# The first MLP layer of a one-core transformer block as seven half-block products for eight

## The chip, the cores and the metric

The kernel runs as one program on one core of a Trainium2 chip. The time is the device time of one execution, in microseconds (us). Five engines work side by side, each with its own queue of instructions in a fixed order: TensorE (PE, the matrix products; PEld is its loading of weights), VectorE (DVE), ScalarE (ACT), GpSimd (POOL) and SyncE (SP), which here only issues DMAs. They wait for each other by semaphores. An instruction that waits holds up all that stands behind it on its engine.

## The reference

One layer of a diffusion backbone: 1024 latent tokens of 1024 features, 256 context tokens. Two mixers (a gated long convolution by a Fourier transform, and retention with eight heads) read the same normed and modulated input, their outputs go through one output projection, and an MLP with a squared ReLU of 4096 hidden features follows:

```python
hx = _modulate(_rmsnorm(x, norm1_g[l]), mx[0][:, None], mx[1][:, None])
ux = hx @ w_in[l]
mix_x = _token_mixers(ux, rope, s_f, s_b, *mixer_w)
x_new = x + mx[2][:, None] * (mix_x @ w_out[l])
hx2 = _modulate(_rmsnorm(x_new, norm2_g[l]), mx[3][:, None], mx[4][:, None])
x_new = x_new + mx[5][:, None] * _sq_relu_mlp(hx2, w_mlp1[l], w_mlp2[l])
return _rmsnorm(x_new, norm_f_g)

def _sq_relu_mlp(h, w1, w2):
    return jnp.square(jax.nn.relu(h @ w1)) @ w2
```

Inputs and outputs are float32.

## The kernel before

Features lie on the 128 partitions, tokens along the free axis; a tile of 128 features by 1024 tokens is 4096 bytes of each partition. Every large operand is split into two float32r parts, the nearest 12-bit part (hi, by a cast on ScalarE) and the rest (lo, by a subtraction on VectorE). A product is then three matmuls (mm3, lines 174 to 177): hi by hi, hi by lo, lo by hi. The moving operand has 512 tokens, the stationary one is a 128 x 128 piece of the weights.

Around the change the work goes in four stages.

1. q, the last piece of the input projection (pq, until 566 us). It reads hxh and hxl, the split input.
2. The output projection. Its convolution share (out_conv, poh0 to poh7) reads mxh and mxl, which split_mix makes from mix_d, eight loads into two buffers mraw of 512 tokens each (lines 1042 to 1048). Its pieces stand between the steps of the retention. The retention share (por) reads mrh and mrl, first for tokens 0 to 511, then for the rest. After each half the second norm follows: squares, a sum over the partitions by TensorE (ptr), a root, a broadcast by TensorE (pb, rB), then modulation into h2h and h2l (lines 1186 to 1219).
3. Layer 1 of the MLP, in 16 blocks f of 256 hidden features: 2 x 128 features, 2 halves of the tokens, 8 pieces of the sum and 3 matmuls, 96 in all. Squared ReLU from PSUM gives fh and fl.
4. Layer 2, interleaved with it: block f of the hidden features times 8 output pieces, 96 matmuls, added to XN, the residual, by one VectorE instruction per output piece. Weights come in slabs of 2048 columns, alternately for layers 1 and 2, by prefetch(). The last block works in token parts of 512, 256 and 256, and the final norm follows part by part.

A scheduler orders the instructions of each engine from the order in which they were written; `with urgent()` moves those within it ahead by a fixed amount. Pools are taken from two stacks of SBUF, a left one from low addresses up and a right one from the top down. A tile that takes the place of an earlier one waits for the last reader of that. In bytes of a partition: hxh and hxl lie at 60,512 to 126,048, h2h and h2l at 89,184 to 154,720, mxh and mxl at 163,808 to 196,576, mrh and mrl at 196,576 to 229,344, fh and fl at 188,384 to 221,152.

In the names of instructions, wr_ and wh_, wl_ are a weight slab raw and split (m: MLP, o: output projection), mod2 the gates and shifts.

## Time and profile before

| | |
|---|---|
| three runs, us | 1441.08, 1443.73, 1448.71; median 1443.73 |
| profiled execution, span, us | 1444.2 (no other time is given for it) |
| busy: PE, DVE, ACT, POOL | 1395.0, 870.6, 393.0, 28.3 us |
| matmuls of PE, listed | 7158 |
| mean granted TensorE clock | 0.982 of full speed |
| DMA | 164.77 MB, mean 114 GB/s |

The span is cut into stages by the timelines: the MLP runs from about 712 to 1427 us, half of the whole. Busy times of PE are sums of matmuls that overlap at their ends, so what one costs in a row of many is read from the distance of two starts. A granted clock of 1.00 is 2.4 GHz, 0.50 is 1.2 GHz.

### The profile page before, as it was taken

The page shows a single profiled execution, that of the slowest core. Times are in us where ns is not written, and L with a number is a line of the kernel's source. Part 1 is how long each engine was busy: PE and PEld are TensorE (multiplying, and loading weights), DVE is VectorE, ACT ScalarE, POOL GpSimd, SP SyncE. Part 2 cuts the span into 40 slices and gives each one's busy share as a digit, 9 for nine tenths or more (in the row PEclk, how much of TensorE's full clock was granted, in tenths as well). Part 3 has the DMA queues.
Part 4 walks back from the last instruction along what each step waited for, and adds up shares of the span by engine and source line. Part 5 has one row for each costly group of instructions (what it writes and reads, how often), then busy time and mean ns, then how long its engine had stood idle before and what let it go on. Part 6 is the DMA issues. An engine that isn't in the chain of part 4 may idle for free.

```text
span 1444.2 us, 17943 instructions
## 1 busy us (share of the span) xinstructions
PE 1395.0 (97%) x7158; PEld 1164.4 (81%) x7158; DVE 870.6 (60%) x1365; ACT 393.0 (27%) x600; POOL 28.3 (2%) x36
## 2 busy tenths in 40 slices
...
GB/s 370 154 153 178 223 191 169 105 207 177 131 140 229 150 228 256 241 142 104 44 15 59 37 51 53 35 59 44 44 59 44 44 59 36 53 51 37 59 15 117
DMA packets 80690, 164.77 MB, mean 114 GB/s; under 512 B 8928, under 2 KB 39264, under 8 KB 80352
## 3 DMA queue, kind: packets, MB, share of 16 engines
...
q0 software_dynamic: 1152, 4.19, 0.7%
...
## 4 chain that ended last, share of the span: by engine, by line
PE 83%; DVE 7%; DMA 5%; ACT 2%; issue 1%; SPq 0%; POOL 0%; DVEq 0%; POOLq 0%; ACTq 0%
PE pm L177 15%; PE pm L176 15%; PE pm L175 15%; PE px L175 2%; PE px L176 2%; PE px L177 2%; PE pga L397 1%; DMA dft_f_k<-in_dft_f 1%; PE pGv L900 1%; PE pq L176 1%; PE pq L177 1%; PE pq L175 1%; PE poh L176 1%; PE poh L177 1%; PE poh L175 1%
## 5 line engine op out<-in xcount | busy, mean ns | idle before, releaser
L1295 DVE SCALAR_TENSOR_TENSOR XN<-pm,mod,XN 128x1024 f32<-128x1024 f32 x120 | 154.0, 1283 | 118.3 <-PE pm L177 118.2
L175 PE MATMUL pm<-fh,wh_m 128*128 128x512 f32 (+1 forms) x528 | 205.2, 389 | 0.3 <-DVE XN L1284 0.2
L177 PE MATMUL pm<-fh,wl_m 128*128 128x512 f32 (+1 forms) x528 | 205.4, 389 | 0.0
L176 PE MATMUL pm<-fl,wh_m 128*128 128x512 f32 (+1 forms) x528 | 204.9, 388 | 0.0
L196 ACT CAST wh_m<-wr_m 128x1024 fp32r<-128x1024 f32 x64 | 67.2, 1050 | 457.8 <-PE pm L176 334.4
L197 DVE TENSOR_TENSOR wl_m<-wr_m,wh_m 128x1024 fp32r<-128x1024 f32 x64 | 78.1, 1221 | 169.9 <-ACT wh_m L196 169.8
L176 PE MATMUL pm<-h2l,wh_m 128*128 128x512 f32 x448 | 174.4, 389 | 0.0
L177 PE MATMUL pm<-h2h,wl_m 128*128 128x512 f32 x448 | 174.3, 389 | 0.0
L175 PE MATMUL pm<-h2h,wh_m 128*128 128x512 f32 x448 | 174.3, 389 | 0.0
L175 PEld LDWEIGHTS pm<-fh,wh_m 128*128 128x128 f32 x528 | 99.1, 188 | 23.5 <-DVE XN L1284 0.7
L177 PEld LDWEIGHTS pm<-fh,wl_m 128*128 128x128 f32 x528 | 99.1, 188 | 22.8 <-issue 0.2
L176 PEld LDWEIGHTS pm<-fl,wh_m 128*128 128x128 f32 x528 | 99.1, 188 | 22.6
L175 PEld LDWEIGHTS pm<-h2h,wh_m 128*128 128x128 f32 x448 | 84.1, 188 | 17.7
L176 PEld LDWEIGHTS pm<-h2l,wh_m 128*128 128x128 f32 x448 | 84.1, 188 | 17.5
L177 PEld LDWEIGHTS pm<-h2h,wl_m 128*128 128x128 f32 x448 | 84.1, 188 | 17.5
L1238 DVE TENSOR_TENSOR rl<-rl 128x1024 f32<-128x1024 f32 (+1 forms) x36 | 39.5, 1101 | 78.9 <-ACT fh L1237 78.9
L175 PE MATMUL px<-hxh,wh_x 128*128 128x512 f32 x128 | 50.7, 396 | 0.0
L176 PE MATMUL px<-hxl,wh_x 128*128 128x512 f32 x128 | 50.7, 396 | 0.0
L712 DVE SCALAR_TENSOR_TENSOR adac<-adaw,cs,adac 128x512 f32<-128x512 f32 x56 | 43.0, 767 | 12.7 <-DMA adaw<-in_w_ada 12.0
L177 PE MATMUL px<-hxh,wl_x 128*128 128x512 f32 x128 | 50.5, 394 | 0.0
L1236 ACT ACTIVATE rl<-pm 128x1024 f32<-128x1024 f32 x28 | 28.7, 1026 | 57.1 <-PE pm L177 57.1
L177 PE MATMUL pk<-wh_k,hxl 128*128 128x256 f32 x128 | 39.6, 310 | 3.2 <-DVE hxl L438 3.2
...
## 6 DMA issues: line engine op xcount, KB each, us to landing
wr_m<-in_w_mlp SPq DMA_DIRECT2D x64, 512.0 KB, 3.5
adaw<-in_w_ada SPq DMA_DIRECT2D x64, 256.0 KB, 4.0
wa<-in_w_ada SPq DMA_DIRECT2D x16, 512.0 KB, 10.2
...
xr<-in_x SPq DMA_DIRECT2D x8, 512.0 KB, 7.2
eo_d<-eo POOLq DMA_DIRECT2D x8, 512.0 KB, 4.3
...
```

The costliest lines, as they stand in the source:

```text
L175: PE.matmul(o, lhsT=lh, rhs=rh, start=first, stop=False)
L176: PE.matmul(o, lhsT=lh, rhs=rl, start=False, stop=False)
L177: PE.matmul(o, lhsT=ll, rhs=rh, start=False, stop=last)
L196: A.copy(wh[:, ks], raw)
L197: V.tensor_tensor(wl[:, ks], raw, wh[:, ks].bitcast(F32), op=ALU.subtract)
L397: PE.matmul(pga[h][0:4, n, :], lhsT=cv[:, k, :], rhs=w_[:, n * 512:(n + 1) * 512], start=(k == 0), stop=(k == KC - 1 and i == 1))
L712: V.scalar_tensor_tensor(ac, wa, cs[:, k, 0:1], ac, op0=ALU.mult, op1=ALU.add)
L900: PE.matmul(o, lhsT=y[:, 0, cb], rhs=iv[:, sl[0]], start=True, stop=False)
L1236: A.activation(rl, ps, AF.Relu)
L1238: V.tensor_tensor(rl, rl, rl, op=ALU.mult)
L1295: V.scalar_tensor_tensor(xn[d], ps.rearrange("p a n -> p (a n)"), gate2[:, d:d + 1], xn[d], op0=ALU.mult, op1=ALU.add)
```

## The change

Layer 1 becomes a product of 2 x 2 blocks. For each f the weights are cut by hidden half (128 features of the first 2048, 128 of the second) and by half of the sum; the activations by half of the sum and by half of the tokens. With A11, A12, A21, A22 for the weights and B11 to B22 for the activations, seven products stand for eight:

- 1: A11 B11; 2: A12 B21; 5: (A21 + A22) T1 with T1 = B12 - B11; 6: (S5 - A11) T2 with S5 = A21 + A22 and T2 = B22 - T1; 3: (A12 - S6) B22; 7: (A11 - A21) T3 with T3 = B22 - B12; 4: A22 T4 with T4 = B21 - T2.

Each is 4 pieces of the sum by 3 matmuls. The weights' sums are made once per f (w1_prep), the tokens' once (b11 to t4, 16,384 bytes each, at 19,552 to 153,568). Copies of PSUM (s1, s5, s2) and additions (join) put the four blocks of the output together. The squared ReLU is stored unsplit to DRAM (h_d). When layer 1 is done, layer 2 loads it back and splits it, in 8 groups of four chunks of 128 hidden features.

Beside this: the second half of the tokens goes through the output projection in two parts of 256; the modulation is done in place in XN, so XN is stored to DRAM (x_d) and loaded again for layer 2; XN moves to the right stack at 196,576, mxh and mxl to 89,184 to 121,952, mrh and mrl to 56,416 to 89,184, hidden tiles to 19,552 to 85,088.

The diff, cut to its core (removed code of the MLP and comments left out):

```diff
+    xnp = opool("xnp", side="right")
+    XN = xnp.tile([P, KC, T], F32, tag="XN", name="XN")
     xn = [XN[:, k] for k in range(KC)]
-    mxr = opool("mxr", side="right")
-    mxp = opool("mxp", side="right")
+    mxr = opool("mxr")
+    mxp = opool("mxp")
...
+    w1p = opool("w1p", side="right")
+    raws = {}
+
+    def w1_load(f):
+        raw = w1p.tile([P, KC, 2, P], F32, tag="raw", name=f"w1r{f}")
+        for h in range(2):
+            SP.dma_start(raw[:, 4 * h:4 * h + 4], I["w_mlp1"][f][:, 4 * h:4 * h + 4])
+        a11, a12, a21, a22 = raw[:, 0:4, 0], raw[:, 4:8, 0], raw[:, 0:4, 1], raw[:, 4:8, 1]
+        raws[f] = dict(a11=a11, a12=a12, a21=a21, a22=a22)
...
+    def w1_split(f, p, a):
+        t = w1[f, p] = w1p.tile([P, 2, 4, P], F32R, tag=f"w{p}", name=f"w1{p}_{f}")
+        split(t[:, 0], t[:, 1], raws[f][a])
+
+    def w1_sum(f, p, a, b, op):
+        r = raws[f]
+        t = w1p.tile([P, 4, P], F32, tag="sum", bufs=3, name=f"w1s{p}_{f}")
+        V.tensor_tensor(t, r[a], r[b], op=op)
+        r[p] = t
+        w1_split(f, p, p)
...
+    b0p = opool("b0p", side="right")
+    n2p = opool("n2p", side="right")
+    B = {}
+
+    def b_tile(pool, key):
+        B[key] = pool.tile([P, 2, 4, 512], F32R, name=f"B_{key}")
+        return B[key][:, 0], B[key][:, 1]
+
+    with urgent():
+        w1_load(0)
+    for p in (1, 2, 5, 6, 3, 7, 4):
+        w1_prep(0, p)
+    b11, b21 = b_tile(b0p, "b11"), b_tile(b0p, "b21")
+    x_d = tc.dram_tile([P, KC, T], F32, name="x_d")
+
     wo = [slabs.pop(("o", 2)), slabs.pop(("o", 3))]
 
...
+    def out_ret(c0, w):
+
+        cc, nt = slice(c0, c0 + w), w // P
+        ss = n2p.tile([P, 512], F32, tag="ss", name=f"ss2{c0}")[:, 0:w]
         for dp in range(4):
-            ps = ps_mm(f"por{h}{dp}")
+            ps = ps_mm(f"por{c0}{dp}")[:, :, 0:w]
             for b in range(2):
                 d = 2 * dp + b
                 wh, wl = wo[d // 4]
                 cb = slice((d % 4) * P, (d % 4 + 1) * P)
                 for k in range(4):
-                    mm3(ps[:, b], wh[:, k, cb], wl[:, k, cb], mrh[k][:, hc_], mrl[k][:, hc_], k == 0, k == 3)
+                    mm3(ps[:, b], wh[:, k, cb], wl[:, k, cb], mrh[k][:, cc], mrl[k][:, cc], k == 0, k == 3)
             for b in range(2):
                 d = 2 * dp + b
                 with urgent():
-                    V.scalar_tensor_tensor(xn[d][:, hc_], ps[:, b], gate1[:, d:d + 1], xn[d][:, hc_],
+                    V.scalar_tensor_tensor(xn[d][:, cc], ps[:, b], gate1[:, d:d + 1], xn[d][:, cc],
                                            op0=ALU.mult, op1=ALU.add)
-                    squares(ss, xn[d][:, hc_], d, n2p, f"m{h}")
-            if h == 1 and dp % 2 == 1:
-                prefetch()
+                    squares(ss, xn[d][:, cc], d, n2p, f"m{c0}")
+            SP.dma_start(x_d[:, 2 * dp:2 * dp + 2, cc], XN[:, 2 * dp:2 * dp + 2, cc])
...
+    def modulated(k, cc, rB2):
+
+        y = xn[k][:, cc]
+        V.scalar_tensor_tensor(y, y, A2[:, k:k + 1], rB2, op0=ALU.mult, op1=ALU.mult)
+        A.activation(y, y, AF.Identity, bias=B2[:, k:k + 1], scale=1.0)
+
+    cc, rB2 = out_ret(0, 512)
+    with urgent():
+        for kh, (hi, lo) in enumerate((b11, b21)):
+            for k2 in range(2):
+                ks = slice(4 * kh + 2 * k2, 4 * kh + 2 * k2 + 2)
+                for k in (ks.start, ks.start + 1):
+                    modulated(k, cc, rB2)
+                split(hi[:, 2 * k2:2 * k2 + 2], lo[:, 2 * k2:2 * k2 + 2], XN[:, ks, cc])
+    parts = [out_ret(512, 256)]
+    parts += [out_ret(768, 256)]
     for d in range(8):
         dbg(f"xn{d}", xn[d])
+    cpool("mxr")
+    cpool("wpool")
+    btp = opool("btp")
+    t2, t1, t3, b22, t4 = [b_tile(btp, key) for key in ("t2", "t1", "t3", "b22", "t4")]
+    for q, (cc, rB2) in enumerate(parts):
+        qs = slice(256 * q, 256 * q + 256)
+        y11, y21, y12, y22 = XN[:, 0:4, qs], XN[:, 4:8, qs], XN[:, 0:4, cc], XN[:, 4:8, cc]
+        with urgent():
+            for k in range(4):
+                modulated(k, cc, rB2)
+                modulated(4 + k, cc, rB2)
+
+            u2 = n2p.tile([P, 4, 256], F32, tag="u2", name=f"u2{q}")
+            for o, a, b in ((y11, y12, y11), (u2, y22, y11), (y21, y21, u2), (y12, y22, y12)):
+                V.tensor_tensor(o, a, b, op=ALU.subtract)
+            for (hi, lo), src in ((t1, y11), (t2, u2), (b22, y22), (t3, y12), (t4, y21)):
+                split(hi[:, :, qs], lo[:, :, qs], src)
     cpool("n2p")
-    cpool("mxr")
...
+    evp = opool("evp", side="right")
+
+    CH = xnp.tile([P, KC, T], F32, tag="XN", name="CH")
+    h_d = [tc.dram_tile([P, T], F32, name=f"h_d{c}") for c in range(2 * NB)]
+    banks = {}
+
+    def product(f, p):
+
+        x = banks[f]["y" if p in (5, 3) else "z" if p == 2 else "x"]
+        w, key = w1.pop((f, p)), {1: "b11", 2: "b21", 3: "b22", 4: "t4", 5: "t1", 6: "t2", 7: "t3"}[p]
+        for k in range(4):
+
+            mm3(x, w[:, 0, k], w[:, 1, k], B[key][:, 0, k], B[key][:, 1, k], p in (1, 2, 5) and k == 0, k == 3,
+                skip_group_check=True)
+
...
+    def join(f, i, j, bank, nm):
+        with urgent():
+            V.tensor_tensor(banks[f][i][:, j], bank, banks[f][nm], op=ALU.add)
+
+    def finish_row(f, i):
+        c = banks[f][i]
+        V.scalar_tensor_tensor(c, c, 0.0, c, op0=ALU.max, op1=ALU.mult)
+        SP.dma_start(h_d[2 * f + i], c.rearrange("p j n -> p (j n)"))
+
+    def step1(f):
+        mlp1_open(f)
+        product(f, 1)
+        snap(f, "s1", banks[f]["x"])
+
+    def step2(f):
+        product(f, 2)
+        join(f, 0, 0, banks[f]["z"], "s1")
+
+    def step5(f):
+        banks[f]["y"] = ps_aux(f"pmy{f}")
+        product(f, 5)
+        snap(f, "s5", banks[f]["y"])
+        w1_prep(f + 1, 5)
+
+    def step6(f):
+        product(f, 6)
+        snap(f, "s2", banks[f]["x"])
+        w1_prep(f + 1, 6)
+
+    def step3(f):
+        product(f, 3)
+        join(f, 0, 1, banks[f]["y"], "s2")
+        w1_prep(f + 1, 3)
+        finish_row(f, 0)
+
+    def step7(f):
+        product(f, 7)
+        join(f, 1, 1, banks[f]["x"], "s5")
+        w1_prep(f + 1, 7)
+
+    def step4(f):
+        product(f, 4)
+        with urgent():
+            A.copy(banks[f][1][:, 0], banks[f]["x"])
+        w1_prep(f + 1, 4)
+        finish_row(f, 1)
+        banks.pop(f)
+
+    with urgent():
+        w1_load(1)
+
+    step1(0)
+    w1_prep(1, 1)
+    step2(0)
+    w1_prep(1, 2)
+    step1(1)
+    step2(1)
+    for f in range(NB):
+        step5(f)
+        step6(f)
+        step3(f)
+        step7(f)
+        if 1 <= f < NB - 1:
+            step1(f + 1)
+        step4(f)
+        if f + 2 < NB:
+            with urgent():
+                w1_load(f + 2)
+            w1_prep(f + 2, 1)
+        if 1 <= f < NB - 1:
+            step2(f + 1)
+        w1_prep(f + 2, 2)
+    cpool("btp")
+    cpool("evp")
+    cpool("b0p")
+    cpool("w1p")
+
...
+    hdp = opool("hdp")
+    w2p = opool("w2p", side="right")
+    NG = NB // 2
+    XN = xnp.tile([P, KC, T], F32, tag="XN", name="XN2")
+    xn = [XN[:, k] for k in range(KC)]
+    for k in range(KC):
+        SP.dma_start(xn[k], x_d[:, k])
+
+    def mlp2_load(g):
+        hid, wts = [], []
+        with urgent() if g else ExitStack():
+            for s in range(2):
+                f = 2 * g + s
+                w = w2p.tile([P, 2, 2, D], F32R, tag="w2", bufs=4, name=f"w2_{f}")
+                for i in range(2):
+                    t = hdp.tile([P, 2, T], F32R, tag="hid", bufs=8, name=f"hid{f}{i}")
+                    raw = hdp.tile([P, T], F32, tag="hraw", bufs=2, name=f"hraw{f}{i}")
+                    SP.dma_start(raw, h_d[2 * f + i])
+                    split(t[:, 0], t[:, 1], raw)
+                    raw = w2p.tile([P, D], F32, tag="w2r", bufs=2, name=f"w2r{f}{i}")
+                    SP.dma_start(raw, I["w_mlp2"][f][:, i])
+                    split(w[:, 0, i], w[:, 1, i], raw)
+                    hid.append(t)
+                    wts.append((w[:, 0, i], w[:, 1, i]))
+        return hid, wts
+
     def part(o, d, cc):
+            db = slice(d * P, (d + 1) * P)
+            for c in range(4):
+                mm3(o, wts[c][0][:, db], wts[c][1][:, db], hid[c][:, 0, cc], hid[c][:, 1, cc], c == 0, c == 3)
...
-    # ------------------------------------------------------------------ final norm, back to token rows
+
+    ahead = mlp2_load(0)
+    for g in range(NG):
+        now, ahead = ahead, mlp2_load(g + 1) if g + 1 < NG else None
+        pair = mlp2(g, *now)
+
```

Three places of the engines' orders, each before and after. A wait names the engine or the DMA queue (DMAHW) that ends it; the number behind it counts the kernel's semaphores.

First, ScalarE where q ends (mraw00 and mraw01 are the two halves of the first of four tiles, wh_o0 and wh_o1 the weights of the output projection). Before:

```order
L196 CAST wh_q1_4896<-wr_q11_4902 128x1024 [waits DMAHW4_49]
L978 ACTIVATE vxl31_4380<-vxl31_4380,cols_84 128x512 [waits DMAHW2_49,DMAHW6_49,DMAHW0_49,DVE_49]
L1047 CAST mxh0_5402<-mraw00_5422 128x512 [waits DMAHW4_49]
L1047 CAST mxh0_5402<-mraw01_5426 128x512 [waits DMAHW6_49]
L196 CAST wh_o0_5132<-wr_o00_5134 128x1024 [waits DMAHW0_49,PE_49,Activation_49]
L1047 CAST mxh1_5403<-mraw10_5430 128x512 [waits DMAHW3_49,DMAHW0_49,Pool_49]
L196 CAST wh_o0_5132<-wr_o01_5138 128x1024 [waits DMAHW7_49]
L1047 CAST mxh1_5403<-mraw11_5434 128x512 [waits DMAHW1_49]
L1047 CAST mxh2_5404<-mraw20_5438 128x512 [waits DMAHW2_49]
L1047 CAST mxh2_5404<-mraw21_5442 128x512 [waits DMAHW5_49]
```

After:

```order
L197 CAST wh_q1_4896<-wr_q11_4902 128x1024 [waits DMAHW4_49]
L971 ACTIVATE vxl31_4380<-vxl31_4380,cols_84 128x512 [waits DMAHW2_49,DMAHW6_49,DMAHW0_49,DVE_49]
L197 CAST wh_o0_5132<-wr_o00_5134 128x1024 [waits DMAHW0_49,PE_49,Activation_49]
L197 CAST wh_o0_5132<-wr_o01_5138 128x1024 [waits DMAHW0_49]
L197 CAST wh_o1_5368<-wr_o10_5370 128x1024 [waits DMAHW5_49,DVE_49,PE_49]
L1040 CAST mxh0_5402<-mraw00_5422 128x512 [waits DMAHW4_49]
L1040 CAST mxh0_5402<-mraw01_5426 128x512 [waits DMAHW6_49]
L197 CAST wh_o1_5368<-wr_o11_5374 128x1024 [waits DMAHW1_49]
L1040 CAST mxh1_5403<-mraw10_5430 128x512 [waits DMAHW3_49]
L1040 CAST mxh1_5403<-mraw11_5434 128x512 [waits DMAHW4_49]
```

The casts of mxh0 and mxh1 stand behind one of wh_o1 that waits for PE, the last products of q; the casts of mxh2 and mxh3 follow later, among the first copies of the retention.

Second, TensorE where the projection passes into layer 1 (pb is the broadcast of the norm, pm1_0 the PSUM tile of f = 0, pmy0 that of its product 5, B_t1 the tile T1, B_b21 the tile B21). Before:

```order
L177 MATMUL pm1_0h0_6871<-h2h3_6423,wl_m10_6440 128x512
L1211 MATMUL pb21_6811<-dg210_6812,ones_83 128x128 [waits DVE_49,PE_49]
L1211 MATMUL pb21_6811<-dg211_6815,ones_83 128x128 [waits DVE_49]
L175 MATMUL pm1_0h0_6871<-h2h4_6424,wh_m10_6439 128x512
L1211 MATMUL pb21_6811<-dg212_6818,ones_83 128x128 [waits DVE_49]
L1211 MATMUL pb21_6811<-dg213_6821,ones_83 128x128 [waits DVE_49]
L176 MATMUL pm1_0h0_6871<-h2l4_6432,wh_m10_6439 128x512
L177 MATMUL pm1_0h0_6871<-h2h4_6424,wl_m10_6440 128x512
L175 MATMUL pm1_0h0_6871<-h2h5_6425,wh_m10_6439 128x512
```

After:

```order
L179 MATMUL pm1_1_7110<-B_b11_6458,w11_1_7091 128x512
L1263 MATMUL pb2768_6955<-dg27680_6956,ones_83 128x128 [waits DVE_49,PE_49]
L1263 MATMUL pb2768_6955<-dg27681_6959,ones_83 128x128 [waits DVE_49]
L177 MATMUL pmy0_7138<-B_t1_6970,w15_0_6437 128x512 [waits Activation_49]
L178 MATMUL pmy0_7138<-B_t1_6970,w15_0_6437 128x512 [waits DVE_49]
L179 MATMUL pmy0_7138<-B_t1_6970,w15_0_6437 128x512
L177 MATMUL pmy0_7138<-B_t1_6970,w15_0_6437 128x512
L178 MATMUL pmy0_7138<-B_t1_6970,w15_0_6437 128x512
L177 MATMUL pm1_0_7076<-B_b21_6459,w12_0_6432 128x512 [waits Activation_49]
L178 MATMUL pm1_0_7076<-B_b21_6459,w12_0_6432 128x512
L179 MATMUL pm1_0_7076<-B_b21_6459,w12_0_6432 128x512
L177 MATMUL pm1_0_7076<-B_b21_6459,w12_0_6432 128x512
```

Before, matmuls of layer 1 on the first half of the tokens stand between the broadcasts of the second. After, five matmuls of product 5, with its waits for ScalarE and VectorE, stand ahead of product 2, and the rest of product 5 behind it.

Third, SyncE between the layers. Before, in the middle of the MLP, where weights of both layers alternate:

```order
L195 DMA wr_m1121_9554<-in_w_mlp1 128x1024 [waits DMAHW4_49,DVE_49]
L195 DMA wr_m2110_9672<-in_w_mlp2 128x1024 [waits DMAHW5_49,DVE_49]
L195 DMA wr_m2111_9676<-in_w_mlp2 128x1024 [waits DMAHW6_49,DVE_49]
L195 DMA wr_m1130_9794<-in_w_mlp1 128x1024 [waits DMAHW7_49,DVE_49]
L195 DMA wr_m1131_9798<-in_w_mlp1 128x1024 [waits DMAHW0_49,DVE_49]
L195 DMA wr_m2120_9916<-in_w_mlp2 128x1024 [waits DMAHW1_49,DVE_49]
```

After, where layer 1 ends (h_d30 and h_d31 are the last stores of hidden rows, hraw00 to hraw11 the first loads of them, w2r weights of layer 2, XN2 the residual):

```order
L1342 DMA h_d30_7071<-CH_7040 128x1024 [waits DVE_49]
L1430 DMA hraw00_9174<-h_d0_7041 128x1024 [waits PE_49]
L1433 DMA w2r00_9178<-in_w_mlp2 128x1024 [waits DMAHW2_49]
L1342 DMA h_d31_7072<-CH_7040 128x1024 [waits DMAHW3_49,DVE_49]
L1430 DMA hraw01_9183<-h_d1_7042 128x1024 [waits DMAHW4_49]
L1433 DMA w2r01_9187<-in_w_mlp2 128x1024 [waits DMAHW5_49]
L1419 DMA XN2_9163<-x_d_6460 128x1024 [waits DMAHW6_49,DMAHW7_49,DMAHW3_49,DMAHW0_49]
L1419 DMA XN2_9163<-x_d_6460 128x1024 x2
L1419 DMA XN2_9163<-x_d_6460 128x1024 [waits DMAHW1_49]
L1419 DMA XN2_9163<-x_d_6460 128x1024 [waits DMAHW2_49]
L1419 DMA XN2_9163<-x_d_6460 128x1024
L1419 DMA XN2_9163<-x_d_6460 128x1024 [waits DMAHW4_49]
```

The next are one more part of XN2 and then hraw10, w2r10, hraw11, w2r11, which wait for DVE to free the two buffers.

## Rows read from the trace of the kernel before

**Rows 1.** Page section 1: engine, busy us (share), instructions

```profile
PE 1395.0 (97%) x7158; PEld 1164.4 (81%) x7158; DVE 870.6 (60%) x1365; ACT 393.0 (27%) x600; POOL 28.3 (2%) x36
```

**Rows 2.** Windows in the MLP: window, length, busy us of each engine, PEclk, DMA share, GB/s

```profile
1350.00:1400.00 50.00, 50.00 (x218) 40.73 (x218) 22.19 (x18) 8.29 (x8) 0.00 (x0) 1.00 0.10 32
```

**Rows 3.** Timeline of PE, layers 1 and 2: start us, length us, instruction

```profile
1002.32 0.39 PE L175 MATMUL pm<-h2h,wh_m 128*128 128x512 f32 x1
...
1024.09 0.40 PE L175 MATMUL pm<-fh,wh_m 128*128 128x512 f32 x1
...
1046.48 0.39 PE L175 MATMUL pm<-h2h,wh_m 128*128 128x512 f32 x1
```

**Rows 4.** Timeline of PE, output projection

```profile
707.82 0.39 PE L176 MATMUL por<-mrl,wh_o 128*128 128x512 f32 x1
...
711.54 0.40 PE L177 MATMUL por<-mrh,wl_o 128*128 128x512 f32 x1
```

**Rows 5.** Timeline of PE, from q to the output projection

```profile
565.46 0.28 PE L176 MATMUL pq<-wl_q,hxh 128*128 128x256 f32 x1
565.58 0.28 PE L177 MATMUL pq<-wh_q,hxl 128*128 128x256 f32 x1
...
566.06 0.47 PE L175 MATMUL poh<-mxh,wh_o 128*128 128x512 f32 x1
```

**Rows 6.** Groups of PE in the MLP: line, shapes, count, busy, mean ns, idle before

```profile
L175 PE MATMUL pm<-fh,wh_m 128*128 128x512 f32 x496 | 195.9, 395 | 0.0
...
L175 PE MATMUL pm_0h<-h2h,wh_m 128*128 128x512 f32 x32 | 12.7, 395 | 1.2 <-DVE XN L1200 1.2
...
L175 PE MATMUL pm<-fh,wh_m 128*128 128x256 f32 x32 | 9.3, 291 | 0.3 <-DVE XN L1284 0.2
```

**Rows 7.** Timeline of DVE, second norm

```profile
691.58 0.16 DVE L1173 TENSOR_SCALAR tvar<-ptr 128x4 f32<-128x4 f32 x1 [1.14 <-PE ptr L1171]
...
704.78 1.22 DVE L197 TENSOR_TENSOR wl_m<-wr_m,wh_m 128x1024 fp32r<-128x1024 f32 x1
705.92 1.41 DVE L1218 SCALAR_TENSOR_TENSOR h2l<-y,mod,h2h 128x512 fp32r<-128x512 f32 x2
707.24 1.41 DVE L1216 SCALAR_TENSOR_TENSOR y<-XN,A,rB 128x512 f32<-128x512 f32 x2
...
711.69 0.68 DVE L1184 TENSOR_TENSOR ss<-ss,sq2m 128x512 f32<-128x512 f32 x1
712.29 0.74 DVE L1200 SCALAR_TENSOR_TENSOR XN<-por,mod,XN 128x512 f32<-128x512 f32 x1
```

**Rows 8.** Window of weight loads at the start

```profile
20.00:36.00 16.00, 16.00 (x57) 4.97 (x56) 9.37 (x13) 9.86 (x15) 0.00 (x0) 1.00 1.03 410
```

**Rows 9.** Instructions of mxh, their first and last start, and their waits

```profile
L1047 ACT CAST mxh<-mraw x8: 619/620/622, 540.0 to 563.4; 128x512 fp32r<-128x512 f32 x8
...
  DMA mraw<-mix_d: 21.1, 6
```

**Rows 10.** Page section 6: DMA issues, count, KB each, us to landing

```profile
XN<-in_xT SPq DMA_DIRECT2D x8, 512.0 KB, 9.5
...
vx_d<-vv SPq DMA_DIRECT2D x4, 512.0 KB, 3.6
...
mraw<-mix_d SPq DMA_DIRECT2D x8, 256.0 KB, 4.6
```

**Rows 11.** Groups of DVE in the MLP

```profile
L1284 DVE SCALAR_TENSOR_TENSOR XN<-pm,mod,XN 128x256 f32<-128x256 f32 x15 | 7.0, 474 | 0.4 <-PE pm L177 0.3
```

**Rows 12.** Page section 5: casts of MLP weights

```profile
L196 ACT CAST wh_m<-wr_m 128x1024 fp32r<-128x1024 f32 x64 | 67.2, 1050 | 457.8 <-PE pm L176 334.4
```

**Rows 13.** Timeline of PE, a pause

```profile
238.34 3.15 PE L783 MATMUL pT<-vt,kw 128*128 128x64 f32 x16 [1.60 <-ACT vt L774]
```

**Rows 14.** Windows behind two pauses

```profile
239.00:249.00 10.00, 10.00 (x49) 10.00 (x48) 2.77 (x4) 2.94 (x8) 0.00 (x0) 0.50 0.38 129
515.40:518.90 3.50, 3.50 (x18) 3.50 (x18) 0.16 (x1) 0.00 (x0) 0.00 (x0) 0.51 0.61 194
```

151 lines of the change are left out of this document (56 added, 95 removed).

## The prediction

> **What bounds the kernel now.** I read the engine shares first: TensorE is busy for 1395.0 us of the span of 1444.2 [rows 1]. A window late in the MLP shows 50.00 of 50.00 us at granted clock 1.00, the upper of the two levels, 2.4 GHz [rows 2]; from 712 to 1400 us TensorE does not pause, so there only the number of matmuls and the time from one start to the next count. The span is what I sum against; the shown runs have their median at 1443.73, 0.5 below it, and no other time is given for the profiled execution.
>
> The durations in the listings overlap (0.39 us each), so the price of a matmul is read from starts. One block of layer 1 runs from 1002.32 to 1024.09 us: 96 matmuls of 512 columns in 21.77 us, 226.8 ns each. The following block of layer 2, from 1024.09 to 1046.48, takes 22.39 us for the same 96, 233.2 ns [rows 3]. What differs is where the moving tile lies: h2h and h2l below byte 154,720 of a partition, fh and fl above 188,384. The output projection, with mrh and mrl above 196,576, agrees: 16 steps from 707.82 to 711.54, 232.5 ns [rows 4]. With 256 columns the step is 0.12 us [rows 5].
>
> **What the change removes.** Layer 1 falls from 16 x 96 = 1536 to 16 x 84 = 1344 matmuls; its new moving tiles end at 153,568, so both kinds cost 226.8 ns: 192 x 0.2268 = 43.5 us. Layer 2 keeps its products. Before, 3 x 496 of 512 columns and 3 x 32 of 256 [rows 6]: 1488 x 0.2332 + 96 x 0.12 = 358.5. Afterwards seven of eight groups and half of the last are of 512 columns, 1440, and 192 of 256, with tiles below 85,088: 1440 x 0.2268 + 192 x 0.12 = 349.6. That is 8.9 less. The convolution share of the output projection, 192 matmuls, gains 1.1; its retention share pays 192 steps of 0.12 for 96 of 0.2325 in the second half and gains nothing. Layer 2 updates the residual half as often, which may free about 1 us of the tail. Together 54.5 us.
>
> The Trainium skill, "SBUF — State Buffer", section "SBUF: two separate sides", says that the engines' ports are apart and PE never waits on anyone; by it the address of a tile would not matter. [Rows 3, 4] show 6 ns, whatever makes them.
>
> **What it adds inside layer 1.** One f now takes TensorE 84 x 0.2268 = 19.05 us. VectorE then has seven splits and four sums of 512 (0.60 each), three joins of 512 from PSUM (0.66) and two squarings of 1024 (1.32): about 11.2 us; ScalarE seven casts and four copies, under 8 us; the DMAs move 2 MB, 5.1 us at 410 GB/s [rows 7, 8]. All this lies under TensorE: nothing.
>
> **What it adds at three seams.** There the work before was hidden and no longer is.
>
> *First seam, q to output projection.* Before, the eight casts of mraw ran from 540.0 to 563.4 us, under the last q matmuls; ScalarE spent 21.1 us of that waiting for their loads [rows 9], and TensorE went from pq at 565.58 to poh at 566.06 without a stop [rows 5]. The change puts mxh and mxl at 89,184 to 121,952, over hx tiles that q still reads. So all eight follow the end of q: in the first order fence a weight cast that waits for TensorE now stands before the first. Two loads are there already; the other six go through two buffers, each pair waiting for the subtraction before it, with 4.6 us from issue to landing [rows 10]: three rounds of about 6 us (4.6, cast 0.62, subtraction 0.6), 18, and 2 for the first pair: 20 us. TensorE has about 11 us to do meanwhile (poh0 and poh1 up to the chunks that are there, and retention's small products): a loss of 9. Bounds: 4 if the loads land in 3 us in place of 4.6 (three rounds of 4.4), 13 if TensorE finds only 7 us of work.
>
> *Second seam, output projection to layer 1.* Before, one wait of 1.2 us [rows 6]. Now VectorE has to make the sums and differences of the tokens and split them. Between the first update from por02 and the low part of B_t1's second half, VectorE's order holds 17 instructions of 1024 elements, 11 updates and 17 additions of 512, 46 of 256, 8 of 128 and 14 tiny ones. In steps from start to start: 1024 costs 1.14 (704.78 to 705.92), two updates of 512 1.32, an addition of 512 0.60 [rows 7]; 256 about 0.38 (0.474 less the overlap of 0.09 that the 512 ones show) [rows 11]; 128 0.24, a tiny one 0.2. 19.4 + 7.3 + 10.2 + 17.5 + 1.9 + 2.8 = 59.1 us, and some 3 in which it waits itself, as for 1.14 at 691.58 behind a norm [rows 7]. TensorE has in that time por03 (24 x 0.2268 = 5.4), the rest of the projection (192 x 0.12 = 23.0), product 1 of f = 0 and 1 (5.4) and 14 small ones (2): 35.9 us. The second order fence shows why it does no more: product 5 of f = 0 (pmy0), which needs B_t1, stands before product 2 of f = 0 and 1, whose 24 matmuls need nothing of it. 59.1 + 3 - 35.9 = 26.2; less the 1.2 of before, plus 1 for w12_1, queued behind B_t2 to B_t4 on VectorE, plus 2 for the clock (below): 28. Bounds: 18, where VectorE does not wait and has the 4.8 us of weight splits behind it; 36, where each of eight splits waits 1 us for ScalarE's cast (1.05 [rows 12]).
>
> *Third seam, layer 1 to layer 2.* The last hidden row is written after the last product and read later; the third order fence shows SyncE's queue there. hraw00 waits for the last product, h_d31 for the squaring (some 2.3 us after it), hraw01 and w2r01 stand behind, then come eight reloads of XN, 4.19 MB. They wait for h_d31 to land, as their place is its source: 3.6 us [rows 10], so about 6.3 us after the last product. They need 10.2 us at 410 GB/s [rows 8], and hraw10, w2r10, hraw11, w2r11, 2.1 MB more, are issued behind them. So chunk 2 is split at about 22 us (6.3 + 10.2 + 2.6 for the next megabyte + 2.2 for cast and subtraction, 1.05 and 1.14 [rows 7, 12], and the issues), chunk 3 at about 26. TensorE meanwhile has chunks 0 and 1 of two outputs, 5.2 us; the order takes all four chunks of an output in turn. Loss 20.5, with the clock 23. Bounds: 15, if hraw10 and hraw11 do not queue behind the reloads; 33, if both pairs take the 9.5 us that a reload of XN took here [rows 10].
>
> What the clock adds is read from two pauses: after 1.60 us without work at 238.34 [rows 13] the granted clock stood at 0.50, the lower level, for 10 us of work; at 515.4 for 3.5 us [rows 14]. The 1.2 us at 711 cost nothing. Half clock for 3.5 us costs 1.7; I put 2 to 2.5 at the longer seams.
>
> **Sum.** 54.5 less 9 + 28 + 23 = 60: 5.5 us slower, 1449.7, less 0.5 for the median: 1449 us. The gain is bounded within 2 us by counts; the losses lie between 37 and 82, hence between 1426 and 1471.
>
> **Rivals.**
> 1. The seams are shorter. All three are hand-walked orders in which I let each wait count in full; loads that overlap, or TensorE's later matmuls falling better, would take a third off. For it: VectorE works 22 of 50 us in the MLP and the DMAs a tenth [rows 2], so much could be done earlier if a wait ends sooner than I let it. Losses of 40: 1443.7 - 54.5 + 40 = 1429.
> 2. Half clock, on the slower side. Place: behind each of the three pauses. Price: if all fall as at 239 to 249 us, 5.1 us each, 15 in place of the 4.5 in my sum; with pauses that end in bits (product 5 starts, stops for the low part, starts) twice that, 30. It decides as soon as the lower level holds beyond the first 3.5 us. 1449 + 10 to 25: about 1466. Against it: the fall at 515.4 lasted 3.5 us. The Trainium skill, "TensorE: Matmul & The Clock Gate", section "Why this matters for your kernels", warns of such gaps between bursts; by it all three pauses would be followed by the lower level, which my sum has for two.
> 3. The 6 ns follow not the address but that fh, fl are written while others are read; then the new hidden tiles, written so too, keep 233.2: 9 + 1 us lost, 1459. Against it: mrh and mrl were complete at 707.82 to 711.54 and cost the same. The skill's sentence on the ports would give this time as well.
> 4. The preparation of weights does bind layer 1: raw has one buffer, so load (3.6), casts and sums follow each other; I see 5 us of room in 19. If 1 us per f is missing: 16, 1465.
>
> **Chances.** My forecast 0.48, rival 1 0.28, rival 2 0.15, rival 3 0.06, rival 4 0.03. 0.5%, 7.2 us, is about what a measurement here can tell from no change: 1436.5 to 1451. The forecast's own spread (1440 to 1458) gives 0.32 within and 0.16 slower; rival 1 gives 0.26 faster and 0.02 within; the others are slower. Faster 0.26, same 0.34, slower 0.40. The range of 1426 to 1469 leaves about one in ten on either side.
>
> **What would show it.** Layer 1 at 19.05 us per f without pauses; steps of 226.8 ns in layer 2; a pause of TensorE of about 9 us among poh0 and poh1, one of about 26 before pmy0 with VectorE busy all along, and one of about 20 in the first outputs of layer 2 with XN's reload moving at 400 GB/s. I am wrong if any of these is under half its size, if pmy0's releaser is another engine, or if layer 2 steps at 233.

## The result, and the profile after

Four runs of the changed kernel have their median at 1462.55 us (1460.54 to 1470.80), four runs of the kernel before at 1445.83 (1441.08 to 1448.71). The ratio, estimated over all of them, is 1.0135, with an interval of 1.0093 to 1.0177 (the two medians alone make 1.0116): slower by 1.35%. The time is 13.6 us above the 1449 of the forecast and inside its range, whether that ends at the 1471 of its sum or at the 1469 stated with the chances. The profiled execution has a span of 1458.6 us against 1444.2, and the lines below are read from it.

The engines' row of the page (answers to [rows 1]): engine, busy us, share, instructions.

```profile
PE 1366.0 (94%) x7110; PEld 1138.9 (78%) x7110; DVE 905.7 (62%) x1519; ACT 444.7 (30%) x736; POOL 28.5 (2%) x36
```

TensorE has 48 matmuls fewer: 192 taken out of layer 1, 96 added in the output projection, 48 in layer 2. It is busy for 29 us less and the kernel is longer, so idle time has come in. That is not all. Two windows in which TensorE does not pause once (answers to [rows 2]: window, length, busy us of each engine and its count, granted clock, DMA share, GB/s):

```profile
800.00:1050.00 250.00, 250.00 (x1082) 202.63 (x1081) 141.84 (x205) 81.63 (x141) 0.00 (x0) 1.00 0.31 106
1100.00:1400.00 300.00, 300.00 (x1293) 243.28 (x1292) 127.61 (x106) 50.76 (x50) 0.00 (x0) 1.00 0.25 86
```

The second lies within layer 2. 300 / 1293 is 232.0 ns from one start to the next at full clock, where the forecast had 226.8. In layer 1 the price depends on the moving tile. These are the first of each twelve matmuls, and one row of layer 2 with the one 96 matmuls later (timeline of TensorE, answers to [rows 3]: start us, length us, instruction):

```profile
904.97 0.39 PE L177 MATMUL pm<-B_b,w 128*128 128x512 f32 x1
...
907.70 0.40 PE L177 MATMUL pmy<-B_t,w 128*128 128x512 f32 x1
...
910.49 0.40 PE L177 MATMUL pm<-B_t,w 128*128 128x512 f32 x1
...
913.29 0.40 PE L177 MATMUL pmy<-B_b,w 128*128 128x512 f32 x1
...
916.09 0.40 PE L177 MATMUL pm<-B_t,w 128*128 128x512 f32 x1
...
1199.62 0.40 PE L177 MATMUL pm<-hid,w 128*128 128x512 f32 x1
...
1221.93 0.39 PE L177 MATMUL pm<-hid,w 128*128 128x512 f32 x1
```

The first is product 2, with the plain block B21 (B_b): 2.73 us, 227.5 ns a matmul. The next two, of the tiles T1 and T2 (B_t), take 2.79 and 2.80, 233 ns, and so does product 3 with B22, which lies beside the T tiles and is named B_b too: 2.80. Layer 2 steps at 232.4 ns. So five of the seven products and all of layer 2 pay the dearer of the two prices of [rows 3], although the tiles lie at low places.

The three seams, in TensorE's timeline (answers to [rows 4 to 6]; in brackets idle us before the instruction and who ended it). First seam:

```profile
560.25 0.50 PE L177 MATMUL poh<-mxh,wh_o 128*128 128x512 f32 x1 [1.22 <-ACT mxh L1040]
...
562.91 0.80 PE L178 MATMUL poh<-mxl,wh_o 128*128 128x512 f32 x1 [2.16 <-DVE mxl L1041]
...
567.58 0.73 PE L177 MATMUL poh<-mxh,wh_o 128*128 128x512 f32 x2 [0.28 <-ACT mxh L1040]
```

Second seam, from the projection's second half to layer 1:

```profile
690.02 0.58 PE L177 MATMUL por<-mrh,wh_o 128*128 128x256 f32 x1 [3.63 <-DVE XN L1253]
690.40 0.41 PE L178 MATMUL por<-mrl,wh_o 128*128 128x256 f32 x1
690.61 0.41 PE L179 MATMUL por<-mrh,wl_o 128*128 128x256 f32 x1
...
714.01 0.58 PE L177 MATMUL por<-mrh,wh_o 128*128 128x256 f32 x1 [4.85 <-DVE XN L1253]
...
736.35 0.46 PE L1263 MATMUL pb<-dg,ones 128*128 128x128 f32 x2 [2.65 <-DVE dg L1262]
737.59 0.80 PE L1263 MATMUL pb<-dg,ones 128*128 128x128 f32 x2 [0.78 <-DVE dg L1262]
745.49 0.79 PE L177 MATMUL pmy<-B_t,w 128*128 128x512 f32 x1 [7.10 <-ACT B_t L1166]
750.09 0.80 PE L178 MATMUL pmy<-B_t,w 128*128 128x512 f32 x1 [3.80 <-DVE B_t L1167]
```

Six pauses add up to 22.8 us. VectorE is what they wait for; in its timeline the elementwise work on tokens stands back to back. The subtraction at 748.82 makes the low part of T1 for the second half of the tokens; it ends at 750.03, and the last pause, which waits for it, ends at 750.09 (answers to [rows 7]):

```profile
747.68 1.22 DVE L1300 TENSOR_TENSOR XN<-XN,u 128x1024 f32<-128x1024 f32 x1
748.82 1.21 DVE L1167 TENSOR_TENSOR B_t<-XN,B_t 128x1024 fp32r<-128x1024 f32 x1
749.95 1.22 DVE L1167 TENSOR_TENSOR B_t<-u,B_t 128x1024 fp32r<-128x1024 f32 x1
```

Third seam, the start of layer 2: TensorE's pauses, and ScalarE's cast on which the long one rests:

```profile
1066.42 0.80 PE L177 MATMUL pm<-hid,w 128*128 128x512 f32 x1 [7.34 <-ACT w L1166]
...
1070.21 0.79 PE L177 MATMUL pm<-hid,w 128*128 128x512 f32 x1 [0.46 <-ACT w L1166]
...
1084.98 0.80 PE L177 MATMUL pm<-hid,w 128*128 128x512 f32 x1 [12.52 <-ACT w L1166]
```

```profile
1082.54 1.04 ACT L1166 CAST hid<-hraw 128x1024 fp32r<-128x1024 f32 x1 [12.38 <-DMA hraw<-h_d]
1083.88 1.04 ACT L1166 CAST w<-w2r 128x1024 fp32r<-128x1024 f32 x1 [0.30 <-DMA w2r<-in_w_mlp]
```

The weight cast at 1083.88 released TensorE. It waited 0.30 us for its own load; before the cast ahead of it its engine had stood for 12.38 us on the load of a hidden row. The windows of these stretches (answers to [rows 14]) show what moved meanwhile, and the clock:

```profile
690.00:712.00 22.00, 19.15 (x136) 18.94 (x136) 18.33 (x40) 10.65 (x20) 0.00 (x0) 0.86 0.38 129
727.00:745.00 18.00, 7.45 (x32) 5.15 (x30) 17.44 (x33) 14.10 (x25) 0.00 (x0) 0.78 0.05 15
745.00:752.00 7.00, 2.71 (x6) 1.81 (x7) 7.00 (x7) 4.05 (x5) 0.00 (x0) 0.50 0.00 0
1066.00:1072.00 6.00, 5.08 (x11) 3.17 (x12) 3.67 (x3) 2.45 (x3) 0.00 (x0) 0.54 0.91 324
1072.00:1085.00 13.00, 0.48 (x3) 0.04 (x2) 1.27 (x2) 2.09 (x2) 0.00 (x0) 0.61 0.95 379
1085.00:1092.00 7.00, 6.96 (x22) 5.14 (x23) 4.83 (x4) 3.14 (x3) 0.00 (x0) 0.75 0.69 222
```

From 727 to 752 us VectorE works for 24.4 of 25 us. From 1072 to 1085 the DMAs move 379 GB/s while TensorE has 0.48 us of work. Behind each of these pauses the clock is at or near its lower level for a while.

### The profile page after: what moved, and what is told of

The parts are those of the page before. It is cut to its first block, busy times and chain, and to the rows that moved or that the text cites. A ratio compares the mean times of both kernels' runs of the same rounds, so it can differ in the third digit from the quotient of the medians.

```text
span 1458.6 us, 18570 instructions
## 1 busy us (share of the span) xinstructions
PE 1366.0 (94%) x7110; PEld 1138.9 (78%) x7110; DVE 905.7 (62%) x1519; ACT 444.7 (30%) x736; POOL 28.5 (2%) x36
## 4 chain that ended last, share of the span: by engine, by line
PE 78%; DVE 9%; DMA 8%; ACT 2%; issue 2%; POOL 1%; SPq 1%; POOLq 0%; DVEq 0%; ACTq 0%
PE pm L177 13%; PE pm L178 13%; PE pm L179 13%; PE pmy L178 2%; PE pmy L179 2%; PE pmy L177 2%; DMA dft_f_k<-in_dft_f 2%; PE px L177 2%; PE px L178 2%; PE px L179 2%; DMA adaw<-in_w_ada 1%; PE pga L390 1%; DMA hraw<-h_d 1%; PE pq L179 1%; PE pGv L893 1%
## 5 line engine op out<-in xcount | busy, mean ns | idle before, releaser
L177 PE MATMUL pm<-hid,w 128*128 128x512 f32 (+1 forms) x544 | 209.9, 386 | 20.5 <-ACT w L1166 20.3
L178 PE MATMUL pm<-hid,w 128*128 128x512 f32 (+1 forms) x544 | 208.8, 384 | 0.0
L179 PE MATMUL pm<-hid,w 128*128 128x512 f32 (+1 forms) x544 | 208.6, 384 | 0.1
L1463 DVE SCALAR_TENSOR_TENSOR XN<-pm,mod,XN 128x1024 f32<-128x1024 f32 x56 | 71.7, 1281 | 141.9 <-PE pm L179 141.9
L177 PEld LDWEIGHTS pm<-hid,w 128*128 128x128 f32 x544 | 103.4, 190 | 43.9 <-ACT w L1166 21.9
L179 PEld LDWEIGHTS pm<-hid,w 128*128 128x128 f32 x544 | 103.0, 189 | 22.7 <-DVE w L1167 1.5
L178 PEld LDWEIGHTS pm<-hid,w 128*128 128x128 f32 x544 | 103.5, 190 | 21.3 <-issue 0.2
L1166 ACT CAST hid<-hraw 128x1024 fp32r<-128x1024 f32 x32 | 33.6, 1049 | 218.7 <-PE pm L179 180.7
L177 PE MATMUL pm<-B_t,w 128*128 128x512 f32 x192 | 76.0, 396 | 0.8 <-DVE CH L1337 0.8
L179 PE MATMUL pm<-B_t,w 128*128 128x512 f32 x192 | 75.8, 395 | 0.0
L178 PE MATMUL pm<-B_t,w 128*128 128x512 f32 x192 | 75.8, 395 | 0.0
L1167 DVE TENSOR_TENSOR w<-w1r,w 128x512 fp32r<-128x512 f32 x48 | 32.9, 686 | 62.9 <-ACT w L1166 62.9
L1341 DVE SCALAR_TENSOR_TENSOR CH<-CH 128x1024 f32<-128x1024 f32 x32 | 39.1, 1221 | 52.2 <-ACT CH L1378 52.2
L1167 DVE TENSOR_TENSOR hid<-hraw,hid 128x1024 fp32r<-128x1024 f32 x32 | 39.1, 1221 | 43.6 <-ACT hid L1166 43.6
L1166 ACT CAST w<-w1s 128x512 fp32r<-128x512 f32 x64 | 39.6, 621 | 42.7 <-DVE w1s L1176 29.3
L705 DVE SCALAR_TENSOR_TENSOR adac<-adaw,cs,adac 128x512 f32<-128x512 f32 x56 | 42.9, 766 | 13.8 <-DMA adaw<-in_w_ada 13.1
L177 PE MATMUL pm<-B_b,w 128*128 128x512 f32 x128 | 50.7, 396 | 0.4 <-ACT w L1166 0.4
L178 PE MATMUL pm<-B_b,w 128*128 128x512 f32 x128 | 50.5, 394 | 0.0
L179 PE MATMUL pm<-B_b,w 128*128 128x512 f32 x128 | 50.3, 393 | 0.2 <-DVE w L1167 0.2
```

What stands on the lines that cost most here:

```text
L177: PE.matmul(o, lhsT=lh, rhs=rh, start=first, stop=False, **kw)
L178: PE.matmul(o, lhsT=lh, rhs=rl, start=False, stop=False, **kw)
L179: PE.matmul(o, lhsT=ll, rhs=rh, start=False, stop=last, **kw)
L705: V.scalar_tensor_tensor(ac, wa, cs[:, k, 0:1], ac, op0=ALU.mult, op1=ALU.add)
L1166: A.copy(hi, src)
L1167: V.tensor_tensor(lo, src, hi.bitcast(F32), op=ALU.subtract)
```

## The experiments

TensorE's matmuls up to the last of q are the same 3184 in all kernels, yet executions differ there by up to 10 us (that matmul starts at 558.3 us in the profile after, at 565.6 in the one before); the granted clock of the first 100 us differs too (0.93 and 0.88). Kernels that ran once are therefore compared by the time from the last q matmul to the end: 878.6 us before, 900.3 after. The change costs 21.7 us there, of which 7.3 don't show in the span, since this execution reached that point earlier. One profile is good to some 3 us here: the changed kernel with 256 unused bytes (below), whose tiles lie at the same places modulo 256 and whose step is the same, takes 897.7, and from the last q to layer 1 the kernels below with the same code there take 166.7 to 169.5.

**What sets 227 or 232?** The places given to the tiles offer a reading that the forecast did not have. Places of the left stack are 96 modulo 256 bytes in both kernels, those of the right stack 224. Where moving and stationary tile agree modulo 256 (h2h and the weights before; mrh and its weights, B11 and B21 and theirs after) the step is 227; where they differ (fh before; T1 to T4, B22 and hid after) it is 232 to 233 on average. This theory is called R in the expectations; A is the forecast's rule, that a low address is cheap, and W is rival 3, that tiles written while others are read are dear. The edit puts 128 bytes under the right stack, so that both stacks agree:

```
+    padp = opool("padp", side="right")
+    padp.tile([P, 32], F32, name="pad")
     filt = opool("filt", side="right")
```

> The changed kernel with 128 unused bytes per partition at the foot of the right stack of SBUF, so that every tile of the right stack lies 128 bytes lower; nothing else. Theory R: a matmul of 512 columns starts 227 ns after the one before it where its moving and its stationary tile leave the same rest modulo 256 bytes, and about 232 where the rests differ. In the trace of the changed kernel: weights and moving tile both in the right stack 227 (B11, B21), both in the left stack 227 (mrh), left with right 232 to 234 (T1 to T4, B22, hidden tiles). With the pad all rests are equal: 960 matmuls of layer 1 lose 6.4 ns, 1440 of layer 2 5.4 ns, together 14 us, ratio 0.990, time about 1448. Rival A, that the byte address itself decides (low is fast): nothing changes, since no tile moves by more than 128 bytes; 1462. Rival W, that tiles written by other engines while the layer runs are slow to read: nothing changes, 1462.

> The kernel before with the same 128 unused bytes at the foot of its right stack. Theory R: fh and fl (right) then have the same rest as their weights (left): 1488 matmuls fall from 233.2 to 226.8 ns, 9.5 us, and the output projection 384 matmuls by 5.7 ns, 2.2 us; about 1434, ratio 0.992. Layer 1 (left with left) stays at 226.8. Rivals A and W: 1446, fh at 233.

The changed kernel with the pad, windows as above:

```profile
800.00:1050.00 250.00, 250.00 (x1105) 207.10 (x1104) 143.92 (x209) 85.02 (x144) 0.00 (x0) 1.00 0.32 112
1100.00:1400.00 300.00, 300.00 (x1325) 248.53 (x1324) 130.37 (x109) 52.57 (x53) 0.00 (x0) 1.00 0.26 87
```

The kernel before with the pad, and without it:

```profile
800.00:1050.00 250.00, 250.00 (x1105) 207.04 (x1104) 114.89 (x94) 47.15 (x46) 0.00 (x0) 1.00 0.15 51
```

```profile
800.00:1050.00 250.00, 250.00 (x1088) 203.82 (x1087) 114.07 (x93) 46.58 (x45) 0.00 (x0) 1.00 0.14 47
```

In full rows both MLPs now step at 226 to 227 ns (250 / 1105 and 300 / 1325; 226.7 from start to start, since a window also counts a matmul that only reaches into it). The changed kernel goes to 1452.50 us (1443.61 to 1456.23; 1.0065 of before, 1.0043 to 1.0088); from the last q to the end it loses 12.2 us, 6.0 of them in layer 1 and 7.1 in layer 2. The kernel before gains too: 1430.56, 0.9915 (0.9887 to 0.9943). The pad moves each right-hand tile by only 128 bytes, and hid is still written while others are read: A and W fall.

Two other sizes of the pad, on the changed kernel:

```
-    padp.tile([P, 32], F32, name="pad")
+    padp.tile([P, 16], F32, name="pad")     # the other kernel: [P, 64]
```

> The changed kernel with 64 unused bytes in place of 128: rests between the stacks then differ by 64 modulo 256 in place of 128. Theory R as it stands asks for equal rests: hidden tiles and T tiles stay at 232 or slower, B11 and B21 at 227. If only a rest modulo 64 mattered, the changed kernel would have no slow pairs at all, so 64 must be short of the period; if the period is 128 bytes, 64 and 128 would differ as here. Rivals A and W: no change.

> Control: 256 unused bytes. Theory R (period 256): all spacings as in the changed kernel, hidden tiles 232, T tiles 233, B11 and B21 227; time about 1461. If the rest modulo 512 or more decides, the spacings change here (to 227 or another value). Rivals A and W: no change.

With 64 bytes:

```profile
1100.00:1400.00 300.00, 300.00 (x1287) 241.60 (x1287) 131.69 (x109) 53.95 (x53) 0.00 (x0) 1.00 0.27 91
```

With 256 bytes:

```profile
1100.00:1400.00 300.00, 300.00 (x1293) 243.25 (x1292) 126.87 (x105) 50.74 (x50) 0.00 (x0) 1.00 0.25 86
```

64 bytes leave the step at 233.1 ns, 256 at 232.0, the count of the changed kernel to the matmul. The times were 1467.14 and 1460.36, one execution each. So it is not that the tiles have moved, nor how far: the step is short at a difference of 0 modulo 256 and long at 64 and 128, the two others tried.

**The seams, one by one, on the padded changed kernel.** First seam, mx tiles in the right stack, where q's operands don't hold them up:

```
-    mxp = opool("mxp")
+    mxp = opool("mxp", side="right")
```

> The changed kernel with the pad of 128 bytes (1452.5 us; from the last q matmul to the end 888.0 us in its trace) and mxh, mxl back in the right stack, off the hx tiles. Theory: the place makes the first seam: from the last q matmul to the first por matmul 103.8 us in the padded kernel, of which 5 to 7 are waits for mxh and mxl and the lower clock behind them; that falls to about 97, the whole by 6 to 7. Rival: the loads of mraw are late anyway, behind XN's on the queue: poh still waits, 102 or more.

The pauses in front of poh are gone, and from the last q to the end it takes 882.0 us, 6.05 less than the padded kernel's 888.0. Between the last q and the first por 11.2 us go (103.8 to 92.6), but 5.0 come back before layer 1 (65.4 to 70.4): 28 small matmuls of the retention now stand behind the first por in place of ahead of it, and the first por pieces come early enough to wait for their own operands (mrh, mrl) and for VectorE's additions, 3.3 us in six pauses. In this pair of profiles the seam is worth 6 us.

Third seam, the reload of XN behind the first loads of layer 2:

```
-    for k in range(KC):
-        SP.dma_start(xn[k], x_d[:, k])
...
-        with urgent() if g else ExitStack():
+        with urgent():
...
     ahead = mlp2_load(0)
+    for k in range(KC):
+        SP.dma_start(xn[k], x_d[:, k])
```

> The padded changed kernel with the reload of XN issued behind the first groups' loads of layer 2 in place of ahead of the third. Theory: the pause of 12.7 us before chunk 2 is bandwidth taken by XN (4.19 MB ahead of hraw10 and w2r10): it falls to 1 to 3 us, the whole by about 11 with the clock. Rival: two raw buffers and the chain load, cast, subtraction set it: the pause stays above 8 us. A third outcome: XN comes too late for the first additions, and TensorE waits for PSUM instead, behind two outputs (a pause of several us some 20 us into layer 2).

```profile
1068.94 0.51 PE L177 MATMUL pm<-hid,w 128*128 128x512 f32 x1 [1.56 <-ACT w L1168]
...
1073.13 0.80 PE L177 MATMUL pm<-hid,w 128*128 128x512 f32 x1 [2.19 <-ACT w L1168]
...
1100.13 0.80 PE L177 MATMUL pm<-hid,w 128*128 128x512 f32 x1 [18.45 <-DVE XN L1462]
```

The pause for the hidden row, 12.0 us in the padded kernel, falls to 1.6 and 2.2, so the reload did cause it. The edit makes the first group's loads urgent as well; the first pause, before chunk 0, stays at 7.27 us (7.36). But now the first update of XN comes late, TensorE runs out of PSUM banks and waits 18.45 us for it: 6.7 us worse in all. The wait is moved, not taken away.

Second seam, product 2 of the first two f given a bank of its own, so that it stands before product 5:

```
-        banks[f] = dict(x=ps[:, 0], z=ps[:, 1])
+        banks[f] = dict(x=ps[:, 0], z=ps_cv(f"z{f}") if f < 2 else ps[:, 1])
```

> The padded changed kernel, where f = 0 and 1 have their product 2 in a PSUM tile of its own, so that it need not wait for the copy of product 1 and stands ahead of product 5. Theory: TensorE's pause before product 5 (7.5 + 4.6 us) is VectorE's work; 14 or more matmuls (3 to 5 us) move into it, and layer 1 with its pauses, 326.1 us, falls by 3 to 5. Rival: VectorE is the bound as far as product 6 and 3, so the time won is lost again behind product 5: under 1 us.

The wait before pmy falls from 7.1 us to 1.06, with 2.49 before product 2 itself; the 3.8 us for the low part stay. Layer 1 with its pauses falls from 326.1 to 323.0 us; from the last q to the end it is 2.8 less.

All three edits together, in ten executions:

> All three edits on the padded changed kernel. If the seams are independent: 6.5 + 11 + 4 = 21 us less than 1452.5, about 1431, ratio to the kernel before 0.992 to 0.994, and level with the padded kernel before (1430.6). If one seam only hands its wait to the next, less: over 1438.

1450.85 us (1446.40 to 1456.93), 1.0053 (1.0028 to 1.0078) of before, which cannot be told from the padded kernel's 1452.50. The XN wait of the late reload, 19.50 us in this profile, eats what the other two give.

**The third seam with its collisions taken apart.** The raw hidden and weight rows get pools of their own, and so other places; the squaring and the store of the last f are urgent, and so are the first group's loads. The reload is urgent too, but a small copy from the fourth weight chunk into XN (overwritten by the reload; the expectation names the hidden row hraw11 loaded just ahead of that chunk) holds it back until that chunk has landed, so that the loads of layer 2 go ahead of it:

```
+    hrwp = opool("hrwp")
     hdp = opool("hdp")
...
+    w2rp = opool("w2rp", side="right")
...
+        with urgent() if f == NB - 1 else ExitStack():
+            V.scalar_tensor_tensor(c, c, 0.0, c, op0=ALU.max, op1=ALU.mult)
...
+                    if (g, s, i) == (0, 1, 1):
+                        V.tensor_copy(XN[:, :, 0:1], raw[:, 0:KC].unsqueeze(2))
...
     ahead = mlp2_load(0)
+    with urgent():
+        for k in range(KC):
+            SP.dma_start(xn[k], x_d[:, k])
```

> The padded changed kernel with the raw tiles of layer 2 (hraw, w2r) in places that come free before the last product of layer 1, and the reload of XN held back by a tiny copy from hraw11, so that it stands behind the first four chunks and ahead of nearly all of the next. Theory (bandwidth and place make the third seam, and XN can come any time before the first output is done, 11 us into layer 2): the pause before layer 2 falls from 7.7 to 2 to 4 us, the one before chunk 2 from 12.7 to under 5, no pause behind it; from the last q to the end 888.0 falls to about 875. Rival: load, cast and subtraction of each chunk in turn bound it: the two pauses together stay above 13. Second rival, as the run before showed: a pause behind the second output, where XN is late; then over 885.

```profile
1058.29 1.22 PE L177 MATMUL pm<-hid,w 128*128 128x512 f32 x2 [3.51 <-ACT hid L1168]
1060.12 0.80 PE L178 MATMUL pm<-hid,w 128*128 128x512 f32 x1 [0.61 <-DVE hid L1169]
...
1068.63 0.50 PE L177 MATMUL pm<-hid,w 128*128 128x512 f32 x1 [0.88 <-ACT w L1168]
```

Of the padded kernel's 19.8 us of pauses some 6 are left, and 870.2 us from the last q to the end are 17.9 less than the padded kernel. Of these, 2.4 lie before layer 1, where this edit changes nothing, so the seam itself is worth about 15.5. One execution took 1433.23 us. How much each of the edits gives was not tried.

**The second seam by the order of the token work.** VectorE makes the tokens' combinations in the order in which the products need them (T1, T2, B22, T3, T4), in place of all sums of a half and then its splits; product 2 has its own bank as above:

```
+            V.tensor_tensor(y11, y12, y11, op=ALU.subtract)
+            part_of(t1, qs, y11)
+            for k in range(4):
                 modulated(4 + k, cc, rB2)
...
+            V.tensor_tensor(u2, y22, y11, op=ALU.subtract)
+            part_of(t2, qs, u2)
```

> The padded changed kernel with product 2 in tiles of its own, and the sums and splits of the tokens written in the order of the products that need them: T1 of both parts first, then T2, B22, T3, T4. VectorE's work is the same, but some 10 us of it (three sums and one split of the first part, three sums and two splits of the second, 9 x 1.14) stand behind T1 in place of ahead. Theory (second seam is VectorE's queue): the pauses before product 5 (1.7 + 4.6 us with product 2 first, 7.5 + 4.6 without) go to under 3, new small ones before products 6 and 7 (2 to 4 us together); layer 1 with its pauses falls from 326.1 (323.0 with product 2 first) to about 315. Rival: the sum of VectorE's work up to T4 is what counts: TensorE waits as long in bits behind products 6 and 7; 321 or more.

```profile
751.50 0.49 PE L177 MATMUL pmy<-B_t,w 128*128 128x512 f32 x1 [0.40 <-ACT B_t L1168]
752.75 0.50 PE L178 MATMUL pmy<-B_t,w 128*128 128x512 f32 x1 [0.76 <-DVE B_t L1169]
```

The two long pauses before product 5 are 0.4 and 0.76 us. Layer 1 falls from 326.1 to 317.1 us, the whole by 11.4; 3.1 of the 9.0 in layer 1 had come with product 2's own bank alone. Small new pauses of 1.08 and 1.50 us stand behind, within product 5 and before product 6.

**All seams and the pad.** The edits of the first, the second (token order) and the third seam (its collisions taken apart) in one kernel, six executions:

> Both, and mxh and mxl in the right stack, on the padded changed kernel. If the three seams are independent: 888.0 - 6 - 13 - 11 = 858 us from the last q to the end, against 868.1 in the padded kernel before; 1452.5 - 30 = about 1422, ratio to the kernel before 0.987. If one hands on its wait to the next: 1432 or more.

```profile
572.76 0.43 PE L1092 MATMUL po<-vtl,sT 128*128 128x64 f32 x2 [1.46 <-DVE sT L1088]
...
715.66 0.58 PE L177 MATMUL por<-mrh,wh_o 128*128 128x256 f32 x1 [5.67 <-DVE XN L1255]
...
1048.73 1.22 PE L177 MATMUL pm<-hid,w 128*128 128x512 f32 x2 [3.51 <-ACT hid L1168]
...
1059.45 0.50 PE L177 MATMUL pm<-hid,w 128*128 128x512 f32 x1 [2.13 <-ACT w L1168]
```

1422.52 us (1419.10 to 1430.36) against 1443.41: 0.9853 (0.9820 to 0.9887). From the last q to the end it takes 860.0 us. The second and the third seam add up: 888.0 less 17.9 and 11.4 is 858.7. The 6 us of the first don't appear beside them: from the last q to layer 1 it takes 167.3 us here and 166.6 in the kernel with the token order alone. Summed from each start to the next, poh and pqd take 5.1 us less than there, but the retention's small products take 2.7 more and por 2.8 more. Of this the trace shows the pause of 1.46 us at 572.76, which VectorE ends, with the granted clock at 0.50 from 574 to 580 behind it, and 8.9 us of pauses among the por matmuls for 7.9. So that seam's wait was moved within the stage and not taken away. Seven products for eight do pay, by 18.6 us off the kernel before from the last q to the end, once the seams are covered and the tiles aligned. Of that the pad alone gives the kernel before 10.6 (868.1): the padded kernel before, 0.9915 (0.9887 to 0.9943), is the fairer rival, and against it the seven products are 8.1 us ahead in the profiles. The two intervals just touch.

## Why the prediction came out as it did

From the last q to the end the forecast's sum was 5.5 us slower; the profile shows 21.7, 16.2 more. Step by step:

- **The price of a matmul, the step that failed.** "Its new moving tiles end at 153,568, so both kinds cost 226.8 ns", and for layer 2 "with tiles below 85,088". The rows had two prices and I tied them to the address because the dear tiles lay high; nothing in [rows 3, 4] set address apart from a difference between the two operands. The forecast called itself wrong "if layer 2 steps at 233": it steps at 232.4. 960 matmuls of layer 1 at 6.4 ns more are 6.1 us, 1440 of layer 2 at 5.6 are 8.1: 14.2 us, and the pad gives 13.1 of them back in the two layers. Rival 3 had the right size for layer 2 and the wrong cause, as the padded kernel shows. The Trainium skill, "SBUF — State Buffer", section "SBUF: two separate sides", has TensorE wait for no other engine. Here the step shifts with no other engine changed, from 232.0 to 226.4 ns by 128 bytes, so that sentence neither forbids nor explains it.
- **The counts.** 192 out, 96 and 48 in: as forecast, by 7158 less 7110. Layer 1 without its pauses takes 34.0 us less (349.1 to 315.1): the 43.5 of the forecast, less the dearer tiles and the lower clock at its start.
- **The work inside layer 1.** Nothing, as forecast: TensorE is busy for 250.00 of 250.00 us. Rival 4 did not happen.
- **First seam.** Pauses of 3.7 us in place of 9: under half, wrong by the forecast's own bound. TensorE found more to do meanwhile than the 11 us I counted: 28 small matmuls (16 of po, 4 of psc, 8 of pz) more than before now stand ahead of the first por. The granted clock fell too, to 0.50 from 563 to 566, for which I had nothing. The stage still costs 6.7 us (TensorE's time from each start to the next, summed over poh and pqd: 53.6 to 60.3), near the 7.9 that 9 less the 1.1 of poh made, and 6.05 by the run with the tiles elsewhere. Right in price, not in form.
- **Second seam.** Pauses of 22.8 us where I had 26.2, with VectorE the last to be waited for and busy for 18.3 of 22 us where the pauses start and 24.4 of 25 where they end: right in place, cause and size. Only not all stood before pmy0: 8.5 us fall on the projection, whose PSUM waits for VectorE's additions, and 10.9 before product 5, whose first releaser is ScalarE's cast of a tile that VectorE had just made: by the letter of the forecast's signs another engine.
- **Third seam.** 20.3 us of pauses for 20.5, 7.34 of them before the first matmul, with the reload at 379 GB/s. Right; some 6 are left of it once the reload is moved and the buffers are freed.
- **The clock.** I gave 2 to 2.5 us to each of the longer seams. The third has 5: 11 matmuls in 6 us, 0.46 of it a pause, and 22 in 7, where at 226.8 ns they would take 2.5 and 5.0. At the second, por's matmuls without the pauses took 51.6 us where they had taken 45.9, 5.7 more where I had nothing, and the matmuls from 727 to 756 some 4 on top. So rival 2 happened, by about 10 us beyond the forecast, the lower end of its 10 to 25; the shorter pauses and the end hide it in the sum.
- **The end.** The last, halved group of layer 2 took 27.2 us where 192 steps of 0.12 made 23.0, but the last block before took 14.6 where I had 11.5 for it: 12.6 more in place of 11.5. The matmuls of the final norm (ptrf, pbf) took 12.2 with their pauses where they had taken 18.6, 6.4 less in place of 1. Together 4.3 less than the forecast.

In the sum: 14.2 for the price, about 8 for the clock at the second seam (5.7 and 4, less the 2 I had), 2.3 for the third seam with its clock, 1.3 for short pauses elsewhere in layer 1 (0.78 of it at its end), less 4.3 for the end, 1.2 for the first seam and 4.4 for the second (3.4 of pauses, 1 for w12_1): about 16, against the 16.2 that were missing. That the price alone comes so near is luck: the other misses, 11.6 up and 9.9 down, happen to cancel. Slower had the largest chance, 0.40; that the value stood within no change is owed to a rule of price drawn from two cases.
